# Pools that stay open across the stages of a two-block kernel, and table work on VectorE alone

## The chip, the cores and the metric

The kernel runs on one core of a Trainium2 chip. The metric is the device time of one execution in microseconds, as the median of several runs. Beside it one execution was recorded by the hardware profiler; all rows below are from that one.

The engines are TensorE (PE; its weight loads, PEld, run beside the matmuls), VectorE (DVE), ScalarE (ACT), GpSimd (POOL), and the DMA engines, which here are fed from the queue of SyncE (SP), in order.

## The reference

One sequence of 512 tokens of width 1024, in float32, goes through two blocks one after the other. What matters here:

```python
# first block
sh1, sc1, gt1, sh2, sc2, gt2 = split(silu(c) @ w_ada + b_ada, 6)     # modulation, w_ada is 1024 x 6144
h = rmsnorm(x, norm1_g) * (1 + sc1) + sh1
z = h @ w_in                                                         # q, k, v of three branches, gates, zs
mix = concat(rmsnorm(nsa_attention(...)), rmsnorm(s5_mixer(zs)))     # attention and a state space mixer
x = x + gt1 * (mix @ w_o)
h = rmsnorm(x, norm2_g) * (1 + sc2) + sh2
a, v = split(causal_dwconv(h @ w_up))                                # 2 x 2816 channels
x = rmsnorm(x + gt2 * ((silu(a) * v) @ w_down), normf_g)
# second block
x = x + short_conv_mixer(rms_norm(x))                                # 1024 -> 4 x 2048 -> 1024
x = x + dilated_attention_mixer(rms_norm(x))                         # 3 groups of 16 heads, gate, output
```

The state space mixer needs tables: powers of a complex number per state (`a_re`, `a_im`), products of these with `b` and with `c`.

## The kernel before, in words

**Matrix products.** Every large product is done in three passes on float32r halves: a value is split into a high part (`xh`, `whi`, a copy that rounds, on ScalarE at line 59) and the rest (`xl`, `wlo`, a subtraction on VectorE, line 95 or 358 or 364), and hi x hi, hi x lo, lo x hi are summed in PSUM. `gemm_b` (matmuls at line 128) puts out channels on partitions, `gemm_a` (line 141) tokens. Weights come in pieces of 512 KB through `wload`: `raw` by DMA (line 109), then `whi` and `wlo`, from a pool `wp` with three buffers of each.

**Stages.** First the modulation columns needed for the first norm, the norm, and a projection to the mixer's input (`tables` and `ada_steps`, with eleven buffers of their own); then the mixer's tables and cores, mixed with the projections to q, k and v in the order that the letters in `ORDER` give; then attention over four query tiles (`attend`, "0" to "3"), the gate of the mixer (G), the output projections (`out_s` is w, `out_a` is x) and more halves of the modulation (j n m e h f i) in the order of `ORDER2`. Then the feed-forward part, the short convolution, and the second attention, each in a pool of its own that holds its normed input `xh`, `xl`, its hidden values `hh`, `hl` and the rest, opened where the one before has been closed.

**Who orders what.** A scheduler orders each engine's instructions at build time, by when they would be ready and by priority: as the program is written, unless a `high_priority` block puts them ahead of all others. Only TensorE's order is the program's in two parts (`manual_schedule`). A tile in a pool waits for the last users of the tiles that were there before it.

**The norm between stages.** `residual` adds a finished bank to `x` and, in the last output projection of a stage, sums the squares. `scaled(g)` turns the sums of half g of the tokens into a factor by some ten small VectorE operations (lines 165 to 175 or 313 to 317) and multiplies (line 323) into two tiles of name `adaw`. `norm_t` transposes these on TensorE (line 350) and writes `xh` and `xl`; the first half ahead, the second inside the next stage's first product (`second`). So a stage starts with its first token half while the other is being made. With `first=True` the same is done for the first norm, in eight turns (four pairs of columns, two token halves), each with two writes of `xl`.

**Modulation.** `ada(which)` takes half of a modulation's columns: four pieces of `w_ada` of 512 KB (line 221) through two buffers of name `adaw`, eight matmuls for each (line 223). The same two buffers serve `w_c1` in `hidden` (line 978) and `scaled`.

**Tables.** `cmul` (lines 706 to 721) is a complex product in six operations. From a width of 8 on the imaginary part's three are on GpSimd. Four groups `h` then build `ti` (lines 777 to 788) and `w1` and `w2` (lines 797 to 804), one of the two factors on GpSimd.

Of the kernel before, what the change touches and what calls it, by code (L numbers as in the profile page):

```python
# [26 lines left out]


ORDER = "kvDBCAKc1lbVda0g"
ORDER2 = "032jGn1mehfwxi"  # L30
TC = dict(schedule_with_timeline_sim=True)


# [10 lines left out]
def f(ap):  # L44
    return ap.bitcast(F32)
# [6 lines left out]
def build(tc, A, out, dump=None, stop=None):  # L52
# [15 lines left out]
    with ExitStack() as top:  # L68
# [142 lines left out]
        xss = cst.tile([128, 2, 4, 4], F32, name="xss")  # L211


        def ada_rows(n0, n1, i0, pool, bufs, at):


            pb = bank(at)
            for i, n in ((i0, n0), (i0 + 1, n1)):
                for r in range(2):
                    raw = pool.tile([128, 1024], F32, name="adaw", bufs=bufs)  # L220
                    dma(raw, A["w_ada"][n][:, r * 1024:(r + 1) * 1024])
                    for q in range(4):
                        mm(pb[32 * q:32 * q + 32, :256], csil[:, r * 4 + q, 3 - i:35 - i], raw[:, q * 256:(q + 1) * 256],  # L223
                           start=i == i0 and r == 0, stop=i > i0 and r == 1)
                    yield pb
# [22 lines left out]
        def ada(which):  # L248

            half = which in asum  # L250
            for pb in ada_rows(which * 4 + 2 * half, which * 4 + 2 * half + 1, 2 * half, b1p, 2, acc):
                pass
            if not half:
                asum[which] = sml.tile([128, 256], F32, name="asum", bufs=3)
                V.tensor_copy(asum[which], pb[:, :256])
            else:
                s = asum[which]
                V.tensor_tensor(s, s, pb[:, :256], op=OP.add)
                if which not in (2, 5):
                    ada_cols(s, range(which * 4, which * 4 + 4), pb[:, 256:])  # L260
# [80 lines left out]
        def norm_t(xh, xl, scale, bias, pool, first=False):  # L341

            def turned(g, kp, xn):
                pt = bank(pst)
                for a in range(2):
                    for q in range(2):
                        k = 2 * kp + a
                        nc.tensor.transpose(pt[:, (2 * a + q) * 128:(2 * a + q + 1) * 128],  # L350
                                            xn[q][:, k * 128:(k + 1) * 128], ident)
                for a in range(2):
                    k = 2 * kp + a
                    src = pt[:, a * 256:(a + 1) * 256]
                    tok = slice(g * 256, (g + 1) * 256)
                    if bias is None:
                        act(xh[:, k, tok], src, AF.Copy, scale=scale[:, k:k + 1])
                        V.scalar_tensor_tensor(xl[:, k, tok], src, scale[:, k:k + 1],
                                               f(xh[:, k, tok]), op0=OP.mult, op1=OP.subtract)
                    else:  # L360
                        t = pool.tile([128, 256], F32, name="ntmp", bufs=4)
                        act(t, src, AF.Identity, scale=scale[:, k:k + 1], bias=bias[:, k:k + 1])
                        act(xh[:, k, tok], t)
                        (P if a and first else V).tensor_tensor(xl[:, k, tok], t, f(xh[:, k, tok]), op=OP.subtract)  # L364

            if first:
                xs = x_normed(pool)
                return lambda kp: [turned(g, kp, xs[g]) for g in range(2)]
            half, twice = ahead.pop()

            with tc.high_priority():
                for kp in range(4):
                    turned(0, kp, half[0])

            def second():

                with tc.high_priority():
                    xn, rf = scaled(1, twice)
                for kp in range(4):
                    turned(1, kp, xn)  # L380
                return half[1], rf
            return second
# [67 lines left out]
        divide(8, "acc", "acc", "acc")  # L450


        with ExitStack() as ph:
            ffp = ph.enter_context(tc.tile_pool(name="ffp", bufs=1, reuse_waits="tile"))
            tmp = ph.enter_context(tc.tile_pool(name="fft", bufs=2, reuse_waits="tile"))
            xh = ffp.tile([128, 8, S], F32R, name="xh")
            xl = ffp.tile([128, 8, S], F32R, name="xl")
            hh = ffp.tile([128, 11, S], F32R, name="hh")
            hl = ffp.tile([128, 11, S], F32R, name="hl")
            taps = ffp.tile([128, 44, 4], F32, name="taps")  # L460
            dma(taps, A["conv_taps"].rearrange("p (a b) -> p a b", a=44))
            gf = ffp.tile([128, D], F32, name="gf")
# [34 lines left out]
        with ExitStack() as ph:  # L497
            cvp = ph.enter_context(tc.tile_pool(name="cvp", bufs=1, reuse_waits="tile"))
            tmp = ph.enter_context(tc.tile_pool(name="cvt", bufs=2, reuse_waits="tile"))
            xh = cvp.tile([128, 8, S], F32R, name="xh")  # L500
            xl = cvp.tile([128, 8, S], F32R, name="xl")
            hh = cvp.tile([128, 8, S], F32R, name="hh")
            hl = cvp.tile([128, 8, S], F32R, name="hl")
            taps = cvp.tile([128, 16, 3], F32, name="taps2")
            dma(taps, A["conv_taps_2"].rearrange("p (a b) -> p a b", a=16))

# [40 lines left out]
def block1_mix(tc, nc, E):  # L547
# [158 lines left out]
    def cmul(orr, oi, ar, ai, br, bi, shape):  # L706
# [8 lines left out]
        TT(orr, a1, a2, op=OP.subtract)  # L715
        a1 = tis[0][:, :16 * w].rearrange("p (g w) -> p g w", g=16)
        a2 = tis[1][:, :16 * w].rearrange("p (g w) -> p g w", g=16)
        e = P if w >= 8 else V
        e.tensor_tensor(a1, ar, bib, op=OP.mult)
        e.tensor_tensor(a2, ai, brb, op=OP.mult)  # L720
        e.tensor_tensor(oi, a1, a2, op=OP.add)

    for m in (1, 2, 4):
        cmul(pr[:, :, m + 1:2 * m + 1], pi[:, :, m + 1:2 * m + 1], pr[:, :, 1:m + 1], pi[:, :, 1:m + 1],
# [49 lines left out]
    for h in range(4):  # L774
        g = slice(h * 4, h * 4 + 4)
        for im in range(2):
# [1 line left out]
            w1 = tb.tile([128, 16, 36], F32, name="w1").rearrange("p a b -> p (a b)")[:, :512].rearrange("p (g n c) -> p g n c", g=4, n=8)  # L778
            w2 = tb.tile([128, 16, 36], F32, name="w2").rearrange("p a b -> p (a b)")[:, :512].rearrange("p (g n c) -> p g n c", g=4, n=8)
            a_ = (pi, pr) if im else (pr, pi)  # L780
            for w, b_, p_, e_ in ((w1, bbr, a_[0], V), (w2, bbi, a_[1], P)):
                e_.tensor_tensor(w, b_[:, g, None, :].to_broadcast([128, 4, 8, 16]),
                                 p_[:, g, 0:8, None].to_broadcast([128, 4, 8, 16]), op=OP.mult)
            (P if im else V).tensor_tensor(ti, w1, w2, op=OP.add if im else OP.subtract)
            pt = bank(pss)
            for q in range(4):
                transpose(pt[:, q * 128:(q + 1) * 128], ti[:, q].rearrange("p n c -> p (n c)"), ident)
# [2 lines left out]
    for h in range(4):  # L790
# [5 lines left out]
        for im in range(2):  # L796
            w1 = tb.tile([128, 16, 36], F32, name="w1").rearrange("p a (b c) -> p (a b c)", b=4).rearrange("p (g n c) -> p g n c", g=4, n=9)
            w2 = tb.tile([128, 16, 36], F32, name="w2").rearrange("p a (b c) -> p (a b c)", b=4).rearrange("p (g n c) -> p g n c", g=4, n=9)
            TT(w1, cr_, pi_ if im else pr_, op=OP.mult)
            P.tensor_tensor(w2, ci_, pr_ if im else pi_, op=OP.mult)  # L800
            TT(w1, w1, w2, op=OP.add if im else OP.subtract)
            for par in range(2):
                s = slice(par * 64, par * 64 + 64)
# [433 lines left out]
    dmp("mixl", f(xl))  # L1237
    if stop != "mix":

        E["ahead"].append((E["scaled"](0), False))  # L1240
        out_a(1)
    ctx.close()

# [12 lines left out]
def block2_attn(tc, nc, E):  # L1256
# [15 lines left out]

    with ExitStack() as ph:
        pp = ph.enter_context(tc.tile_pool(name="a2", bufs=1, reuse_waits="tile"))
        yh = pp.tile([128, 8, S], F32R, name="yh")
        yl = Planes([None] * 8)
        xh = pp.tile([128, 8, S], F32R, name="xh")
        xl = pp.tile([128, 8, S], F32R, name="xl")
        second = norm_t(xh, xl, cols[:, 24:32], None, None)

        wz = wload(A["w_z"][0], 8, 256)
# [11 lines left out]
        dma(gains, A["qk_gain"])  # L1293
        TS(gains[:, 0:3], gains[:, 0:3], -0.125, None, op0=OP.mult)

        kbh = [pp.tile([128, 4, 2, 128], F32R, name=f"kbh{i}") for i in range(2)]
        kbl = [pp.tile([128, 4, 2, 128], F32R, name=f"kbl{i}") for i in range(2)]
        for t in kbh + kbl:
            P.memset(f(t), 0.0)
        md = dr.tile([512, 4], F32, name="md")  # L1300
        wd = dr.tile([512, 2], F32, name="wd")

# [460 lines left out]
```

## Time and profile before

| | us |
|---|---|
| median of 3 runs | 1817.91 (1816.0 to 1825.29) |
| the profiled execution | 1823.86 |
| its span, first to last instruction | 1822.1 |
| TensorE busy in the span | 1751.0 |
| VectorE busy | 1095.5 |
| ScalarE busy | 845.7 |
| GpSimd busy | 184.3 |

A "busy" TensorE has an instruction in it; its granted clock is listed beside it, 1.00 being the full 2.4 GHz. The profiler's span starts at 0; all times in the rows are from there. Idle time is named by what ended it: "[3.80 <-DVE adaw L323]" says that the engine stood 3.80 us until VectorE's instruction of line 323 had written `adaw`.

### The profile page before, as it was taken

What the parts mean: (1) busy time and instruction counts of PE and PEld (TensorE: products, weight loads), DVE (VectorE), ACT (ScalarE), POOL (GpSimd) and SP (SyncE); (2) the same over time, 40 slices, a digit from 0 to 9 for tenths busy, and PEclk for the clock granted to TensorE, in tenths of its full rate; (3) what the DMA queues carried; (4) which work ended last, traced back from release to release, by engine and by line L of the source; (5) the groups of instructions that cost most, each with busy time, mean ns of one, the idle gap of its engine ahead of it and who ended that gap; (6) DMA issues with size and microseconds to landing.
All of it is one profiled execution on the core that took longest, in us unless ns stands there. A gap on an engine that the chain in (4) does not pass through costs nothing.

```text
span 1822.1 us, 25899 instructions
## 1 busy us (share of the span) xinstructions
PE 1751.0 (96%) x9588; PEld 1441.2 (79%) x9588; DVE 1095.5 (60%) x2720; ACT 845.7 (46%) x1679; POOL 184.3 (10%) x179
## 2 busy tenths in 40 slices
PE   5899989999999999899999999999999999999999
PEld 3787746888888888788888888878888888888877
DVE  8895766865545557643333333644766766666676
ACT  3532656564423445532322323445655655656653
POOL 3764202001100110000000000000000000000000
PEclk9998999999999999999999999999999999999999
DMA  8357750332333335333333323533222322322221
GB/s 341 95 152 199 230 176 12 102 122 92 94 92 104 95 102 173 106 104 95 102 93 99 98 93 104 152 107 102 85 78 82 94 73 80 91 74 91 82 65 64
DMA packets 86782, 200.21 MB, mean 110 GB/s; under 512 B 32000, under 2 KB 36864, under 8 KB 86656
## 3 DMA queue, kind: packets, MB, share of 16 engines
q1 hardware_dynamic: 86656, 198.57, 35.3%
q8 instruction: 75, 1.23, 0.3%
q14 instruction: 51, 0.42, 0.1%
HBM read 193.75 MB, written 4.78 MB: 109 GB/s over the span
## 4 chain that ended last, share of the span: by engine, by line
PE 85%; DVE 7%; DMA 4%; ACT 2%; issue 1%; POOL 1%; SPq 0%; DVEq 0%; ACTq 0%; POOLq 0%
PE bank L128 38%; PE bank L141 35%; DMA adaw<-in_w_ada_dram 2%; DVE wlo L95 1%; PE bank L1163 1%; PE bank L1500 1%; PE bank L1470 1%; PE bank L1580 1%; PE bank L223 1%; PE bank L1159 1%; PE bank L1558 1%; PE bank L1140 1%; PE bank L1569 1%; PE bank L1587 1%; ACT whi L59 1%
## 5 line engine op out<-in xcount | busy, mean ns | idle before, releaser
L95 DVE TENSOR_TENSOR wlo<-raw,whi 128x1024 fp32r<-128x1024 f32 (+1 forms) x287 | 350.1, 1220 | 302.5 <-ACT whi L59 288.5
L59 ACT ACTIVATE whi<-raw 128x1024 fp32r<-128x1024 f32 (+1 forms) x287 | 299.4, 1043 | 473.7 <-PE bank L128 265.2
L128 PE MATMUL bank<-xh,whi 128*128 128x512 f32 (+1 forms) x1120 | 291.2, 379 | 10.7 <-ACT xh L59 10.6
L128 PE MATMUL bank<-xl,whi 128*128 128x512 f32 (+1 forms) x1120 | 288.3, 375 | 7.0 <-DVE xl L364 6.8
L128 PE MATMUL bank<-xh,wlo 128*128 128x512 f32 (+1 forms) x1120 | 283.6, 374 | 0.0
L128 PEld LDWEIGHTS bank<-xh,whi 128*128 128x128 f32 x1120 | 204.3, 191 | 52.8 <-ACT xh L59 13.8
L128 PEld LDWEIGHTS bank<-xl,whi 128*128 128x128 f32 x1120 | 203.9, 189 | 47.1 <-DVE xl L364 8.8
L128 PEld LDWEIGHTS bank<-xh,wlo 128*128 128x128 f32 x1120 | 202.4, 189 | 37.7
L141 PE MATMUL bank<-whi,xh 128*128 128x512 f32 (+2 forms) x800 | 209.2, 361 | 2.5 <-ACT v L59 1.2
L141 PE MATMUL bank<-wlo,xh 128*128 128x512 f32 (+2 forms) x800 | 205.1, 356 | 0.0
L141 PE MATMUL bank<-whi,xl 128*128 128x512 f32 (+2 forms) x800 | 204.9, 355 | 0.0
L141 PEld LDWEIGHTS bank<-wlo,xh 128*128 128x128 f32 x800 | 135.5, 190 | 22.5 <-issue 1.6
L141 PEld LDWEIGHTS bank<-whi,xl 128*128 128x128 f32 x800 | 135.2, 190 | 22.5 <-issue 1.6
L141 PEld LDWEIGHTS bank<-whi,xh 128*128 128x128 f32 x800 | 128.8, 189 | 21.2 <-issue 3.9
L141 PE MATMUL bank<-wlo,hh 128*128 128x512 f32 x304 | 95.0, 389 | 0.0
L141 PE MATMUL bank<-whi,hl 128*128 128x512 f32 x304 | 94.9, 389 | 0.0
L198 DVE SCALAR_TENSOR_TENSOR cy<-bank,taps,cy 128x384 f32<-128x384 f32 (+3 forms) x176 | 72.9, 477 | 32.5 <-ACT cy L59 32.5
L59 ACT ACTIVATE P<-P,stat 128x128 f32<-128x128 f32 (+1 forms) x192 | 79.8, 419 | 21.9 <-DVE stat L1478 15.7
L141 PE MATMUL bank<-whi,hh 128*128 128x512 f32 x304 | 89.8, 389 | 0.0
L534 POOL TENSOR_TENSOR cy<-cy,sz 128x512 f32<-128x512 f32 x16 | 28.8, 1801 | 436.5 <-ACT sz L59 436.5
L141 PEld LDWEIGHTS bank<-whi,hl 128*128 128x128 f32 x304 | 57.1, 188 | 11.9
L141 PEld LDWEIGHTS bank<-wlo,hh 128*128 128x128 f32 x304 | 57.0, 188 | 11.8
(384 smaller groups left out, 2322.3 us busy)
## 6 DMA issues: line engine op xcount, KB each, us to landing
raw<-in_conv_w_in_dram SPq DMA_DIRECT2D x64, 512.0 KB, 3.7
raw<-in_w_pair_dram SPq DMA_DIRECT2D x64, 512.0 KB, 3.8
adaw<-in_w_ada_dram SPq DMA_DIRECT2D x48, 512.0 KB, 5.1
raw<-in_w_up_dram SPq DMA_DIRECT2D x44, 512.0 KB, 3.7
raw<-in_w_down_dram SPq DMA_DIRECT2D x30, 512.0 KB, 3.5
raw<-in_conv_w_out_dram SPq DMA_DIRECT2D x24, 512.0 KB, 3.7
raw<-in_w_o_dram SPq DMA_DIRECT2D x12, 512.0 KB, 4.2
x<-in_x_dram SPq DMA_DIRECT2D x8, 512.0 KB, 5.2
```

Of the source, the lines that this page charges most:

```text
L59: return nc.scalar.activation(o, i, fn, **kw)
L95: (eng or V).tensor_tensor(lo, src, f(hi), op=OP.subtract)
L128: mm(ps[:, tok], a[:, q, j * 128:(j + 1) * 128], b[:, k0 + q, tok], start=n == 0 and i == 0 and h != 1, stop=n == len(w) - 1 and i == 3 * ...
L141: mm(ps, a[:, base + k0 + q, tok], b[:, q, :], start=first and n == 0 and i == 0 and o == 0, stop=last and n == len(w) - 1 and i == 3 * kn ...
L198: V.scalar_tensor_tensor(o, i, t, o, op0=OP.mult, op1=OP.add)
L223: mm(pb[32 * q:32 * q + 32, :256], csil[:, r * 4 + q, 3 - i:35 - i], raw[:, q * 256:(q + 1) * 256], start=i == i0 and r == 0, stop=i > i0 ...
L534: P.tensor_tensor(y, y, sz, op=OP.mult)
L1140: mm(ps[:, :n], qs[:, h, qt], kk[:, br, kvh, 0:n], start=kk is ksh, stop=kk is ksl)
L1159: transpose(pt[:, s * 128:(s + 1) * 128], prs[hl][:, j * 128:(j + 1) * 128], ident)
L1163: mm(po[par * 64:par * 64 + 64, kvh * 256:(kvh + 1) * 256], vsw[:, j, br, kvh * 64:kvh * 64 + 64], ptt[:, par, :], start=False, stop=br == ...
L1470: mm(ps[:, :nk * 256], a[:, natural(i)], b[:, j0:i + 1].rearrange("p j h k -> p (j h k)"), start=n == 0, stop=n == 2)
L1500: mm(ps[:, r * 256:(r + 1) * 256], a[:, natural(2 * rr + r)], b[:, 2 * rr + r].rearrange("p h k -> p (h k)"), start=n == 0, stop=n == 2)
```

## The change

Six things are done:

- `xh`, `xl` of the three later stages come from one pool `nx` and `hh`, `hl` (eight planes each) from one pool `hp`, both open from the end of the first block's mixer to the end. The feed-forward part's last three planes are tiles of its own. The second attention uses `hh`'s tile for `yh` and `hl`'s for its four block matrices, zeroed by one instruction.
- The second of each pair of `w_ada` pieces in `ada` goes through `wp`'s `raw` buffers.
- In `ORDER2` the half i stands in front of w and x.
- `scaled(0)` in front of `out_a(1)` has high priority.
- All `xl` of the first norm are made by VectorE, with high priority.
- `cmul` and the tables run on VectorE alone.

```diff
-ORDER2 = "032jGn1mehfwxi"
+ORDER2 = "032jGn1mehfiwx"
...
-        def ada_rows(n0, n1, i0, pool, bufs, at):
+        def ada_rows(n0, n1, i0, pool, bufs, at, more=None):
...
-                    raw = pool.tile([128, 1024], F32, name="adaw", bufs=bufs)
+                    raw = more.tile([128, 1024], F32, name="raw") if more and r else \
+                        pool.tile([128, 1024], F32, name="adaw", bufs=bufs)
...
-            for pb in ada_rows(which * 4 + 2 * half, which * 4 + 2 * half + 1, 2 * half, b1p, 2, acc):
+            for pb in ada_rows(which * 4 + 2 * half, which * 4 + 2 * half + 1, 2 * half, b1p, 2, acc, W["p"]):
...
-                        (P if a and first else V).tensor_tensor(xl[:, k, tok], t, f(xh[:, k, tok]), op=OP.subtract)
+                        with tc.high_priority() if first else nullcontext():
+                            V.tensor_tensor(xl[:, k, tok], t, f(xh[:, k, tok]), op=OP.subtract)
...
+        hp = top.enter_context(tc.tile_pool(name="hp", bufs=1, reuse_waits="tile"))
+        nx = top.enter_context(tc.tile_pool(name="nx", bufs=1, reuse_waits="tile"))
+
+        def hidden():
+            return [hp.tile([128, 8, S], F32R, name=n) for n in ("h0", "h1")]
+
+        def normed():
+            return [nx.tile([128, 8, S], F32R, name=n) for n in ("nxh", "nxl")]
...
-            xh = ffp.tile([128, 8, S], F32R, name="xh")
-            xl = ffp.tile([128, 8, S], F32R, name="xl")
-            hh = ffp.tile([128, 11, S], F32R, name="hh")
-            hl = ffp.tile([128, 11, S], F32R, name="hl")
+            xh, xl = normed()
+            hh, hl = (Planes([h[:, k] for k in range(8)] + [ffp.tile([128, S], F32R, name=f"{n}{k}") for k in range(3)])
+                      for n, h in zip(("hh", "hl"), hidden()))
...
-            xh = cvp.tile([128, 8, S], F32R, name="xh")
-            xl = cvp.tile([128, 8, S], F32R, name="xl")
-            hh = cvp.tile([128, 8, S], F32R, name="hh")
-            hl = cvp.tile([128, 8, S], F32R, name="hl")
+            xh, xl = normed()
+            hh, hl = hidden()
...
-        e = P if w >= 8 else V
-        e.tensor_tensor(a1, ar, bib, op=OP.mult)
-        e.tensor_tensor(a2, ai, brb, op=OP.mult)
-        e.tensor_tensor(oi, a1, a2, op=OP.add)
+        TT(a1, ar, bib, op=OP.mult)
+        TT(a2, ai, brb, op=OP.mult)
+        TT(oi, a1, a2, op=OP.add)
...
-            for w, b_, p_, e_ in ((w1, bbr, a_[0], V), (w2, bbi, a_[1], P)):
-                e_.tensor_tensor(w, b_[:, g, None, :].to_broadcast([128, 4, 8, 16]),
+            for w, b_, p_ in ((w1, bbr, a_[0]), (w2, bbi, a_[1])):
+                TT(w, b_[:, g, None, :].to_broadcast([128, 4, 8, 16]),
...
-            (P if im else V).tensor_tensor(ti, w1, w2, op=OP.add if im else OP.subtract)
+            TT(ti, w1, w2, op=OP.add if im else OP.subtract)
...
-            P.tensor_tensor(w2, ci_, pr_ if im else pi_, op=OP.mult)
+            TT(w2, ci_, pr_ if im else pi_, op=OP.mult)
...
-        E["ahead"].append((E["scaled"](0), False))
+        with tc.high_priority():
+            E["ahead"].append((E["scaled"](0), False))
...
-        yh = pp.tile([128, 8, S], F32R, name="yh")
+        yh, kb = E["hidden"]()
...
-        xh = pp.tile([128, 8, S], F32R, name="xh")
-        xl = pp.tile([128, 8, S], F32R, name="xl")
+        xh, xl = E["normed"]()
...
-        kbh = [pp.tile([128, 4, 2, 128], F32R, name=f"kbh{i}") for i in range(2)]
-        kbl = [pp.tile([128, 4, 2, 128], F32R, name=f"kbl{i}") for i in range(2)]
-        for t in kbh + kbl:
-            P.memset(f(t), 0.0)
+        P.memset(f(kb), 0.0)
+        kbs = [kb[:, 2 * i:2 * i + 2].rearrange("p a (b h k) -> p (a b) h k", b=2, h=2) for i in range(4)]
+        kbh, kbl = kbs[0:2], kbs[2:4]
```

## Rows read from the trace of the kernel before

**Rows 1.** The page: busy time of the engines, and the chain that ended last.
```profile
PE 1751.0 (96%) x9588; PEld 1441.2 (79%) x9588; DVE 1095.5 (60%) x2720; ACT 845.7 (46%) x1679; POOL 184.3 (10%) x179
...
PE 85%; DVE 7%; DMA 4%; ACT 2%; issue 1%; POOL 1%; SPq 0%; DVEq 0%; ACTq 0%; POOLq 0%
```

**Rows 2.** Stretches: length, busy by engine, granted clock, DMA share, GB/s.
```profile
20.00:105.00 85.00, 72.90 (x525) 55.94 (x526) 75.23 (x144) 40.88 (x77) 55.24 (x48) 1.00 0.50 169
105.00:200.00 95.00, 87.67 (x756) 76.58 (x757) 67.84 (x123) 29.86 (x69) 45.73 (x51) 0.91 0.72 199
200.00:262.00 62.00, 54.85 (x396) 32.69 (x394) 45.77 (x174) 36.42 (x96) 5.92 (x8) 1.00 0.61 205
...
340.00:384.00 44.00, 39.22 (x325) 36.86 (x325) 38.22 (x104) 24.29 (x60) 0.00 (x0) 0.96 0.53 170
...
745.00:770.00 25.00, 17.00 (x121) 16.10 (x121) 15.58 (x42) 13.29 (x28) 0.00 (x0) 0.86 0.20 62
...
1194.00:1216.00 22.00, 18.50 (x124) 16.49 (x123) 11.72 (x33) 9.32 (x21) 3.64 (x4) 0.92 0.24 79
```

**Rows 3.** Timeline of VectorE at 23 to 46: start, length, line, operation.
```profile
23.60 0.43 DVE L364 TENSOR_TENSOR xl<-ntmp,xh 128x256 fp32r<-128x256 f32 x1
...
28.20 1.22 DVE L95 TENSOR_TENSOR wlo<-raw,whi 128x1024 fp32r<-128x1024 f32 x1
...
45.84 0.68 DVE L782 TENSOR_TENSOR w<-bbr,pi 128x512 f32<-128x512 f32 x1
```

**Rows 4.** VectorE's groups by form, 20 to 105: busy, mean ns, idle before.
```profile
L95 DVE TENSOR_TENSOR wlo<-raw,whi 128x1024 fp32r<-128x1024 f32 x9 | 14.0, 1553 | 0.2 <-ACT whi L59 0.2
...
L364 DVE TENSOR_TENSOR xl<-ntmp,xh 128x256 fp32r<-128x256 f32 x8 | 7.2, 907 | 0.3 <-ACT xh L59 0.3
L782 DVE TENSOR_TENSOR w<-bbr,pr 128x512 f32<-128x512 f32 x4 | 4.5, 1114 | 2.5 <-POOL ti L784 2.5
```

**Rows 5.** TensorE's waits, whole span: us in total, times, longest.
```profile
PE bank L128 <- DVE xl L364: 6.8, 4, 2.5
...
PE bank L981 <- DMA adaw<-in_w_c_dram: 3.0, 1, 3.0
```

**Rows 6.** TensorE's waits in the stretch 200 to 262.
```profile
PE bank L223 <- DMA adaw<-in_w_ada_dram: 6.8, 8, 1.5
```

**Rows 7.** The load queue (SP), 205 to 262.
```profile
218.97 41.18 SPq L221 DMA_DIRECT2D adaw<-in_w_ada_dram  x15
```

**Rows 8.** Timeline into the feed-forward part, 360 to 380.
```profile
363.20 0.15 DVE L307 TENSOR_REDUCE nss<-xss 128x2 f32<-128x8 f32 x1
...
371.72 0.88 DVE L406 SCALAR_TENSOR_TENSOR rtmp<-bank,rs_yo,gt 128x256 f32<-128x256 f32 x2
...
374.58 1.42 DVE L323 TENSOR_SCALAR adaw<-x,rs_yn 128x1024 f32<-128x1024 f32 x2
...
375.48 3.28 PE L350 MATMUL bank<-ident,adaw 128*128 128x128 f32 x16 [3.80 <-DVE adaw L323]
```

**Rows 9.** Timeline into the convolution, 730 to 768.
```profile
732.36 1.47 PE L350 MATMUL bank<-ident,adaw 128*128 128x128 f32 x12
...
750.96 0.46 ACT L59 ACTIVATE xh<-bank,cols 128x256 fp32r<-128x256 f32 x1
...
751.47 1.22 PE L128 MATMUL bank<-xh,whi 128*128 128x256 f32 x4 [6.27 <-ACT xh L59]
...
751.83 0.48 DVE L358 SCALAR_TENSOR_TENSOR xl<-bank,cols,xh 128x256 fp32r<-128x256 f32 x1
...
757.37 1.42 DVE L323 TENSOR_SCALAR adaw<-x,rs_ym 128x1024 f32<-128x1024 f32 x2
...
763.72 1.91 PE L350 MATMUL bank<-ident,adaw 128*128 128x128 f32 x16
```

**Rows 10.** Timeline into the second attention, 1196 to 1204.
```profile
1198.86 0.17 DVE L1294 TENSOR_SCALAR qkg<-qkg 128x3 f32<-128x3 f32 x1 [1.96 <-DMA qkg<-in_qk_gain_dram]
...
1200.26 0.75 PE L128 MATMUL bank<-xh,whi 128*128 128x256 f32 x4 [2.15 <-ACT xh L59]
```

## The prediction

> **What bounds the kernel now.** I read the page first, then stretches, then waits, then the stages where they collect. TensorE is busy 1751.0 of 1822.1 us and 85% of the chain that ended last is its matmuls [rows 1]: most of the span is matrix work that this change doesn't touch. What it can move is the 71.1 us in which TensorE is idle, and the time at the lower clock. The table of stretches [rows 2] says where they lie: 12.1 us idle in 20 to 105 (tables, first norm, first projection), 7.3 in 105 to 200 with a granted clock of 0.91, 7.2 in 200 to 262 (attention with the modulation weights), 4.8 in 340 to 384 (into the feed-forward part), 8.0 in 745 to 770 (into the convolution), 3.5 in 1194 to 1216 (into the second attention). The first 20 us are the first load and stay. The rows also show VectorE at 75.23 of 85 us in the first stretch with GpSimd at 55.24 beside it, so moving GpSimd's work there isn't free by itself.
>
> **Tables and first norm on VectorE.** By the code 40 GpSimd operations move: each of the norm's eight turns gives one of its two `xl` to GpSimd (a=1), 8 in all; 8 of `w2` and 4 of `ti` with 512 columns; 8 of `w2` with 576; and 12 of `cmul` (three each at 128, 256 and 512 columns, three at 256 for `bbi`). On a free VectorE 256 columns take 0.43 us and 512 take 0.68 [rows 3]; from these I estimate 0.3 for 128 and 0.77 for 576. Sum: 8 x 0.43 + 12 x 0.68 + 8 x 0.77 + 3 x (0.3 + 0.43 + 0.68 + 0.43) = 23.3 us more for VectorE.
> Against it stands a refund. The same forms run longer while GpSimd runs: the `xl` take 0.907 on average where 0.43 was possible, the weight splits 1.553 for 1.22, the first `w1` 1.114 for 0.68 [rows 3, 4]. That is 8 x 0.48 + 9 x 0.33 + 4 x 0.43 = 8.5 us from three groups alone; the other groups are not all shown, so 8.5 is the least and 23.3 (each moved operation already costs VectorE its length today) the most. VectorE also stops waiting for GpSimd (2.5 us before the `w1` group [rows 4]) and has 85 - 75.23 = 9.8 us idle.
> A rule of the Trainium skill bears on it (SBUF — State Buffer, Who interferes with whom): a VectorE instruction with two SBUF inputs and a GpSimd instruction that reads SBUF use one shared read interface, and the later one blocks for the whole length of the other. By that rule the refund is near its upper end and the price near nothing; the rows above would then give a gain of the 6.8 us named next.
> What it does to TensorE: four waits for `xl` cost 6.8 us [rows 5]. The half of `xl` on VectorE stands behind table work there, and the other half behind GpSimd's slower copy of it. With all on VectorE in front of the tables these go. Bounds: -6.8 if the tables end no later; at the other end 23.3 - 8.5 - 9.8 = +5.0, if the least refund is all there is and the tables' consumers wait for it. I take -3, nearer to the gain, since three groups of many already refund a third.
>
> **More load buffers.** `ada` loads four 512 KB pieces a half through two buffers; now every second piece takes one of the three `raw` buffers of the weight loads. In 200 to 262 TensorE waits 6.8 us in eight places for these pieces [rows 6], and the load queue issues 15 of them over 41.18 us [rows 7], one each time a buffer is given back, while the DMA engines are 61% busy [rows 2]. With four or five in flight most waits should go. Bounds: -6.8, and 0 if the softmax between them only moves up to be the next wait. I take -5. Work stays the same; only issue times move. The queue is SP's, in order: a piece that waits for a `raw` buffer holds the weight loads behind it. In 200 to 262 only `w_o` pieces, needed later, are behind; in 105 to 200 (half l) the loads of `w_in_g`, `w_glu` and `w_c` are. There the wait of 3.0 us for `w_c`, which shares the two buffers with l's four pieces [rows 5], should go as l needs two of them. Bounds: -6 (the wait and as much again of the work done at the lower clock in that stretch [rows 2]) and +3 (the same wait, moved to a weight load). I take -2.
> The half i moved ahead of `out_s` and `out_a` costs the same matmuls and loads; it is covered by the same attention work and frees the two buffers that `scaled` needs.
>
> **Into the feed-forward part.** The scale chain starts at 363.20 and its last operation at 374.58: 11.4 us for some ten operations of 0.2 us, because residuals and splits lie between. TensorE's transposes wait 3.80 us for it [rows 8]. At high priority it is done before 370. Next late is the last read of the old PSUM banks, 371.72 + 0.88 = 372.6, which the newly divided PSUM must wait for and this change leaves. So 375.48 moves to 372.6: -2.9, I take -3. Bounds: 0 (a third wait) and -5 (if the 3.28 us for 16 transposes, done in 1.91 elsewhere [rows 8, 9], also falls).
>
> **Into the convolution.** The first token half is transposed by 733.8, but ScalarE writes `xh` only at 750.96, past the last matmul of the down projection, and TensorE stands 6.27 us [rows 9]. `xh` comes from a pool opened where the feed-forward pool is closed; with `nx` kept, only the up projection's matmuls read those bytes before, and by the code they are done before the second down projection starts. Then the first half's matmuls run right behind, and the end is set by the second half: its scaling ends at 757.37 + 1.42, with eight `xl` of 0.48 us, which now are done earlier, in front [rows 9]. 758.8 - 3.8 = 755.0, and 763.72 moves there: -8.7. The least is -3 (half of the 6.27, if the chain of residuals moves no earlier). I take -7, since another 1 to 2 us may stay in the queue order.
>
> **Into the second attention.** TensorE's wait of 2.15 us follows VectorE's 1.96 us for the load of `qkg` [rows 10], a tile in a pool that now begins elsewhere, on bytes free long before. PSUM is divided again here as before, so the transposes still start after the last residual. I take -2, bounds 0 and -4. The one zeroing of `kb` is off the path: its first reader comes some 20 us later.
>
> **The sum.** -3 - 5 - 2 - 3 - 7 - 2 = -22. The profiled execution took 1823.86 us, 1822.1 of it span; 1801.9 is expected of it. The median shown is 1817.91, 5.95 below this execution, so 1817.91 - 22 = 1795.9: I say 1796. All bounds at their best give -6.8 - 6.8 - 6 - 5 - 8.7 - 4 = -37 (1781), all at their worst +5 + 0 + 3 + 0 - 3 + 0 = +5 (1823).
>
> **Rivals.**
> A. As summed, 0.62: 1796, own range 1786 to 1806.
> B. All waits go and the clock stays up, 0.12: 1781. For it speaks the refund and that TensorE is full outside these stretches; against it that each wait has a next one.
> C. The boundaries alone bring something, 0.15: tables and loads hand their gain to VectorE's softmax (45.77 of 62 us busy in 200 to 262 [rows 2]). -3 - 7 - 2 = -12: 1806.
> D. The kept pools do nothing, 0.07: `xh` is late since ScalarE's queue has the squares and splits in front of it, not for its memory. Then 7 and 2 are missing: -13, 1805. Against it: ScalarE writes `xh` directly behind work that waits for the last matmul, 17 us after the transposes.
> E. Slower, 0.04: VectorE saturates. No refund and no usable idle time: the tables end 23.3 us later, TensorE stands behind them at `kq` and the block matrices, and does as much work after it at the lower clock, at which 16 transposes took 3.28 us for 1.91 [rows 8, 9]: 23.3 x (1 - 1.91 / 3.28) = 9.7 us lost. 23.3 + 9.7 - 12 - 5 = +16: 1834. It decides from the point where the tables are over 17 us late, the 12 and 5 of the other gains; with the least refund and the idle time they are 5.0 late. The Trainium skill has a rule that would favour it (Perfetto Trace Analysis, Optimizing Scalar/DVE Operations): where VectorE is saturated, giving work to GpSimd may pay. It adds itself that the two share a read port, so that it might not; the rows on the refund agree with that.
>
> **Chances.** 0.5% (9.1 us, 1808.8) is about what a measurement of this kernel can tell from no change. A, B and most of C and D lie below it: faster 0.85, same 0.11, slower 0.04. The range leaves out part of B below and part of C, D and E above: 1782 to 1809.
>
> **What would show it.** Right: the waits for `xl` and for the modulation pieces gone from the waits of TensorE; `xh` of the convolution written directly behind its transposes, some 10 us ahead of the down projection's last matmul rather than 6 behind it; TensorE's idle time near 745 down to 1 to 3 us; forms on VectorE at 0.43, 0.68 and 1.22 us up to where rope's GpSimd work begins. Wrong: VectorE over 80 of 85 us in the first stretch with a new wait of TensorE for `kq` or `ti`, SP's queue standing on a `raw` buffer in 105 to 200, or `xh` still behind the last matmul.

## The result and the profile after

The changed kernel takes 1795.38 us, median of four runs (1790.6 to 1801.5), against 1821.6 for the kernel before beside it (four runs, 1816.0 to 1826.2): a ratio of 0.9852, 95% interval 0.9828 to 0.9875, or 26.2 us less. The profiled execution of after is the slowest of its four (1801.5 us, span 1799.7); against the profiled one of before (span 1822.1) it is 22.4 us shorter. Executions of one kernel differ by some 10 us: of after's four the fastest had a granted clock of 0.995 over its span and the slowest, the profiled one, 0.988 (before's profiled one 0.991).

The page of after, busy time of the engines and the chain that ended last; they answer to [rows 1]:
```profile
PE 1742.1 (97%) x9588; PEld 1440.5 (80%) x9588; DVE 1095.9 (61%) x2760; ACT 843.4 (47%) x1679; POOL 134.7 (7%) x136
...
PE 86%; DVE 8%; ACT 2%; DMA 2%; issue 1%; SPq 0%; POOL 0%; DVEq 0%; ACTq 0%
```
VectorE executes 40 instructions more than before and is busy 0.4 us more: all the work moved to it is paid back.

The stretches of after, columns as in [rows 2]; the last three are the same boundaries, 13, 19 and 22 us earlier than in before:
```profile
20.00:105.00 85.00, 78.30 (x617) 61.21 (x618) 81.98 (x198) 44.48 (x86) 8.04 (x8) 0.90 0.54 185
105.00:200.00 95.00, 87.56 (x711) 76.50 (x703) 65.75 (x132) 28.45 (x66) 44.52 (x52) 0.91 0.70 207
200.00:262.00 62.00, 59.51 (x464) 37.43 (x463) 45.80 (x171) 37.52 (x99) 5.83 (x8) 0.97 0.64 216
327.00:371.00 44.00, 37.92 (x299) 37.68 (x298) 39.18 (x106) 24.81 (x61) 0.00 (x0) 0.92 0.42 126
726.00:751.00 25.00, 21.33 (x150) 19.44 (x149) 15.84 (x39) 12.76 (x24) 0.00 (x0) 1.00 0.37 107
1172.00:1194.00 22.00, 19.75 (x136) 17.55 (x135) 13.78 (x34) 10.33 (x22) 3.52 (x1) 1.00 0.33 106
```
TensorE gains in all stretches but two. From 105 to 200 it idles as long as before. Into the feed-forward part (327 to 371) it idles 6.1 us where it idled 4.8. The granted clock from 20 to 105 was 0.90 here and 1.00 in before, so that some of the busy time in that stretch is slower matmuls; their number still rose from 525 to 617.

VectorE's groups by form in 20 to 105 of after, against [rows 4]:
```profile
L95 DVE TENSOR_TENSOR wlo<-raw,whi 128x1024 fp32r<-128x1024 f32 x11 | 14.5, 1317 | 0.3 <-ACT whi L59 0.3
...
L366 DVE TENSOR_TENSOR xl<-ntmp,xh 128x256 fp32r<-128x256 f32 x16 | 6.0, 418 | 0.0
...
L790 DVE TENSOR_TENSOR w<-bbr,pr 128x512 f32<-128x512 f32 x4 | 2.8, 692 | 0.1
```
Sixteen `xl` now cost VectorE 6.0 us, where eight cost 7.2 before.

TensorE's waits over the whole span of after, and in a second view those from 200 to 262, against [rows 5, 6]:
```profile
PE bank L224 <- DMA adaw<-in_w_ada_dram: 14.9, 5, 12.2
PE bank L351 <- DVE adaw L324: 8.4, 2, 6.1
PE bank L989 <- DMA adaw<-in_w_c_dram: 2.8, 1, 2.8
PE bank L128 <- ACT nxh L59: 2.7, 4, 1.0
```
```profile
PE bank L224 <- DMA adaw<-in_w_ada_dram: 2.3, 2, 1.3
```
The waits for `xl` are gone (0.2 us left of 6.8), and those for modulation pieces in attention fell from 6.8 to 2.3. The wait for `w_c` is as long as before (2.8, before 3.0), but not the same one (below), and the one for `adaw` into the feed-forward part grew.

The timeline into the feed-forward part of after, against [rows 8]:
```profile
350.57 0.15 DVE L308 TENSOR_REDUCE nss<-xss 128x2 f32<-128x8 f32 x1
...
357.46 1.23 DVE L95 TENSOR_TENSOR wlo<-raw,whi 128x1024 fp32r<-128x1024 f32 x1 [0.97 <-ACT whi L59]
...
358.60 0.48 DVE L408 SCALAR_TENSOR_TENSOR rtmp<-bank,rs_yo,gt 128x256 f32<-128x256 f32 x1
...
361.52 1.41 DVE L324 TENSOR_SCALAR adaw<-x,rs_yn 128x1024 f32<-128x1024 f32 x2
...
362.41 3.64 PE L351 MATMUL bank<-ident,adaw 128*128 128x128 f32 x16 [6.08 <-DVE adaw L324]
```
The scale chain still takes 11 us from its first operation (350.57) to its last (361.52). TensorE's last matmul ended at 356.3, and the reading of its bank stands behind a weight split that itself waits for ScalarE.

The timelines into the convolution (first three) and into the second attention (last), against [rows 9, 10]:
```profile
719.53 1.47 PE L351 MATMUL bank<-ident,adaw 128*128 128x128 f32 x12
...
720.06 1.57 ACT L59 ACTIVATE nxh<-bank,cols 128x256 fp32r<-128x256 f32 x4
...
743.33 2.10 PE L351 MATMUL bank<-ident,adaw 128*128 128x128 f32 x16 [2.33 <-DVE adaw L324]
```
```profile
1178.02 0.50 PE L128 MATMUL bank<-nxh,whi 128*128 128x256 f32 x2 [0.46 <-ACT nxh L59]
```
`nxh` is written right behind its transposes, not 17 us later. Four marks divide the gain of the two profiled executions: the transposes into the feed-forward part are 13.1 us earlier (375.48 to 362.41), the first ones into the convolution 12.8 (732.36 to 719.53), the second ones 20.4 (763.72 to 743.33), and the second attention's first matmul 22.2 (1200.26 to 1178.02). By the prediction's terms these are 13, 13, 20 and 22.

### The profile page after: what moved, and what is told of

Same layout as the page of the kernel before. It is cut to its first block, busy times and chain, and to the rows that moved or that the text cites. A ratio compares the mean times of both kernels' runs of the same rounds, so it can differ in the third digit from the quotient of the medians.

```text
span 1799.7 us, 25866 instructions
## 1 busy us (share of the span) xinstructions
PE 1742.1 (97%) x9588; PEld 1440.5 (80%) x9588; DVE 1095.9 (61%) x2760; ACT 843.4 (47%) x1679; POOL 134.7 (7%) x136
## 4 chain that ended last, share of the span: by engine, by line
PE 86%; DVE 8%; ACT 2%; DMA 2%; issue 1%; SPq 0%; POOL 0%; DVEq 0%; ACTq 0%
PE bank L128 38%; PE bank L141 36%; DVE wlo L95 1%; PE bank L1477 1%; PE bank L1171 1%; PE bank L1507 1%; PE bank L1148 1%; PE bank L1587 1%; PE bank L1167 1%; PE bank L1565 1%; ACT whi L59 1%; DVE h L1462 1%; PE bank L1576 1%; PE bank L1594 1%; DMA adaw<-in_w_ada_dram 1%
## 5 line engine op out<-in xcount | busy, mean ns | idle before, releaser
L128 PE MATMUL bank<-nxh,whi 128*128 128x512 f32 (+1 forms) x1072 | 273.2, 375 | 2.7 <-ACT nxh L59 2.7
L128 PE MATMUL bank<-nxl,whi 128*128 128x512 f32 (+1 forms) x1072 | 271.8, 373 | 0.0
L128 PE MATMUL bank<-nxh,wlo 128*128 128x512 f32 (+1 forms) x1072 | 269.3, 373 | 0.0
L128 PEld LDWEIGHTS bank<-nxh,whi 128*128 128x128 f32 x1072 | 194.8, 189 | 39.4 <-ACT nxh L59 3.8
L128 PEld LDWEIGHTS bank<-nxl,whi 128*128 128x128 f32 x1072 | 194.4, 188 | 35.8
L128 PEld LDWEIGHTS bank<-nxh,wlo 128*128 128x128 f32 x1072 | 193.4, 188 | 35.5
L141 PE MATMUL bank<-whi,nxh 128*128 128x512 f32 x512 | 164.3, 401 | 1.2 <-ACT v L59 1.1
L141 PE MATMUL bank<-whi,h 128*128 128x512 f32 x576 | 160.4, 391 | 0.0
L141 PE MATMUL bank<-whi,nxl 128*128 128x512 f32 x512 | 158.7, 391 | 0.0
L141 PE MATMUL bank<-wlo,nxh 128*128 128x512 f32 x512 | 158.3, 390 | 0.0
L141 PEld LDWEIGHTS bank<-whi,h 128*128 128x128 f32 x576 | 107.5, 188 | 22.2 <-issue 0.2
```

The lines of the kernel that those rows point to most:

```text
L128: mm(ps[:, tok], a[:, q, j * 128:(j + 1) * 128], b[:, k0 + q, tok], start=n == 0 and i == 0 and h != 1, stop=n == len(w) - 1 and i == 3 * ...
L141: mm(ps, a[:, base + k0 + q, tok], b[:, q, :], start=first and n == 0 and i == 0 and o == 0, stop=last and n == len(w) - 1 and i == 3 * kn ...
```

## The experiments

Times are medians, ratios are to the kernel before measured beside each kernel, and a difference to after is taken to its 1795.38. The kernel before itself came out between 1820.42 and 1823.53 in the rounds of the experiments, so that a difference to after of under 3 us says nothing.

**One part alone.** Three kernels carry one part of the change each.

e1, only the work moved to VectorE:
```
-                        (P if a and first else V).tensor_tensor(xl[:, k, tok], t, ...)
+                        with tc.high_priority() if first else nullcontext():
+                            V.tensor_tensor(xl[:, k, tok], t, ...)
-        e = P if w >= 8 else V
-        e.tensor_tensor(a1, ar, bib, op=OP.mult)
+        TT(a1, ar, bib, op=OP.mult)
...
```


> The kernel before with only the table and first-norm operations moved from GpSimd to VectorE (and the first norm's xl ahead in the order). Full refund (the two engines only took each other's time): VectorE's forms at 0.42, 0.68 and 1.22 us, TensorE's projection begins 8 us earlier (before 74.20, after 65.75) and the whole is 5 to 8 us faster. Part refund, as the prediction summed: 3 us faster. Given back: the projection begins earlier, but the wait for w_c and the work at the lower clock behind it take it back by 195 us, and the whole is within 2 us of before.

1818.18 us against 1823.53, ratio 0.9969 (0.9956 to 0.9983). The projection begins at 64.33, 9.9 us earlier than in before, but the transposes into the feed-forward part only 5.3 earlier (370.15): half is given back on the way, and from 200 to 262 TensorE still waits 6.1 us for modulation pieces, at a granted clock of 0.86. The full refund holds: 40 instructions more on VectorE cost it 1.2 us (1095.5 before, 1096.7 here).

e2, only the kept pools:
```
-            xh = ffp.tile([128, 8, S], F32R, name="xh")
-            xl = ffp.tile([128, 8, S], F32R, name="xl")
+            xh, xl = normed()
...
```


> The kernel before with only the kept pools (normed and hidden tiles, one zeroing of kb). Boundaries set by the opening of a pool: xh of the convolution is written right behind its transposes, the wait of 6.27 us goes, TensorE's wait for qkg of 2.15 us goes, and the whole is 7 to 10 us faster. Rival, ScalarE's own order holds xh back: the 6.27 us stay and the whole is within 2 us of before.

1813.07 us, ratio 0.9946 (0.9928 to 0.9965). The timeline of this kernel into the convolution:
```profile
729.02 1.57 ACT L59 ACTIVATE nxh<-bank,cols 128x256 fp32r<-128x256 f32 x4
...
752.29 2.10 PE L350 MATMUL bank<-ident,adaw 128*128 128x128 f32 x16 [2.33 <-DVE adaw L323]
```
With nothing else changed `nxh` is written from 729.02 on, 12 us ahead of the end of the down projection (741.2), and the 6.27 us are gone. What is left, 2.33, is the second half's scale chain. Rival D (ScalarE's order) falls.

e3, only the load buffers, half i's place and the priority:
```
-ORDER2 = "032jGn1mehfwxi"
+ORDER2 = "032jGn1mehfiwx"
-                    raw = pool.tile([128, 1024], F32, name="adaw", bufs=bufs)
+                    raw = more.tile([128, 1024], F32, name="raw") if more and r else \
+                        pool.tile([128, 1024], F32, name="adaw", bufs=bufs)
...
```


> The kernel before with only the raw buffers for the modulation weights, half i ahead of out_s and out_a, and scaled(0) at high priority. By the prediction's terms: 10 us faster (5 in attention, 2 for w_c, 3 into the feed-forward part). By the marks of the two profiles: 9 us gained by the end of attention, 2 to 3 lost again into the feed-forward part, where TensorE's wait for adaw grows from 3.8 to about 6; the whole 5 to 7 us faster. Rival, the softmax takes the place of the loads: 0 to 3 us faster.

1813.45 us, ratio 0.9942 (0.9921 to 0.9964): 10.1 us, the prediction's sum for this part, though not by its terms. TensorE's waits over the whole span in this kernel:
```profile
PE bank L351 <- DVE adaw L324: 6.1, 1, 6.1
...
PE bank L982 <- DMA adaw<-in_w_c_dram: 2.5, 1, 2.5
```
The waits for modulation pieces from 200 to 262 fall by 5.0 to 1.8, a wait for `w_c` is there as in after, and the one into the feed-forward part grows by 2.3 with this part alone. These waits make up less than half of the 10.1; where the rest lies isn't settled. The three parts give 5.4, 10.5 and 10.1, together 25.9; the whole change gave 26.2. They add up.

**What the tables' gain is made of.** e5 moves only the first norm's `xl` (first lines of e1's diff), e6 only the table work (the rest). The high priority around `xl` doesn't put them in front, here or in e1 or after: the kernel compiled without it is the same, instruction for instruction. So e5 tests the engine of half of the `xl`, and no run tests their place in the order.

> The kernel before with only the first norm's xl all on VectorE and ahead in the order; the table work stays on GpSimd. If the gain of the tables part comes from the two engines no longer lengthening each other: VectorE's xl stay near 0.9 us (0.907 before), its weight splits near 1.5, only part of TensorE's 6.8 us of waits for xl goes, and the whole is 1 to 3 us faster. Rival, the place of xl in the order does it: the 6.8 us go and the whole is 5 to 6 us faster, as with the tables moved too.

1824.82 us against 1821.73, ratio 1.0028 (1.0010 to 1.0045): slower. VectorE's `xl` in 20 to 105, TensorE's waits there, and from the timelines of before and of e5 the last `xl`, which in both stand right behind the table product `w<-bbr,pi`:
```profile
L365 DVE TENSOR_TENSOR xl<-ntmp,xh 128x256 fp32r<-128x256 f32 x16 | 12.7, 818 | 0.0
```
```profile
PE bank L128 <- DVE xl L365: 7.7, 5, 2.9
```
```profile
66.18 2.15 DVE L364 TENSOR_TENSOR xl<-ntmp,xh 128x256 fp32r<-128x256 f32 x2
```
```profile
66.61 4.33 DVE L365 TENSOR_TENSOR xl<-ntmp,xh 128x256 fp32r<-128x256 f32 x4
```
All on VectorE, each still takes 0.818 while GpSimd does table work, and TensorE waits 7.7 us for them, not less than the 6.8 of before.

> The kernel before with only the table work moved to VectorE; the first norm keeps every second xl on GpSimd. If the engines lengthen each other: VectorE's forms fall to 0.43 to 0.5 for xl, 1.25 for the weight splits and 0.68 for 512 columns, VectorE's busy time in the first 105 us does not rise by more than 4 us, and the whole is 3 to 5 us faster. Rival, the place of xl: TensorE's waits for xl stay at 5 to 7 us and the whole is within 1 us of before.

1814.52 us, ratio 0.9967 (0.9952 to 0.9982): all of e1's gain. TensorE's waits for `xl` from 20 to 105 in this kernel:
```profile
PE bank L128 <- DVE xl L364: 3.1, 3, 1.8
PE bank L128 <- POOL xl L364: 2.4, 1, 2.4
```
`xl` on VectorE falls only to 0.687, not to the expected 0.43 to 0.5, with the other half still on GpSimd, and 5.5 us of waits are left. So the gain is in the table work's engine; but it is there although most of the waits for `xl` stay, and these go only with both moved (e1, after). How the gain reaches TensorE in e6 isn't settled.

**The load buffers.** e9 is after with `more` left out of the call of `ada_rows`.
```
-            for pb in ada_rows(..., b1p, 2, acc, W["p"]):
+            for pb in ada_rows(..., b1p, 2, acc):
```


> The kernel after without the raw buffers for the modulation weights (two buffers again, half i still moved ahead). If the buffers bring the gain of the loads part (10.1 us alone): TensorE's waits for modulation pieces are back at 18 to 20 us with the start, and the whole is 8 to 11 us slower than after, about 1805. Rival, the moved half i brings it: the whole within 2 us of after.

1810.23 us, 14.9 more than after. TensorE's waits for modulation pieces are 18.6 with the start, 5.9 of them from 200 to 262 (after: 2.3), and the wait into the feed-forward part is 6.81. The buffers carry the gain of their part, though the waits for pieces explain only 3.6 of it. 14.9 is more than the 10.1 of the part alone; whether half i's new place costs the difference when it has two buffers, no run separates.

**Into the feed-forward part.** e4 is after with half i back in its old place.
```
-ORDER2 = "032jGn1mehfiwx"
+ORDER2 = "032jGn1mehfwxi"
```


> The kernel after with half i put back behind out_s and out_a(0). If i's matmuls and its place covered the scale chain: TensorE's wait for adaw into the feed-forward part falls from 6.08 to 4 us or less, and the whole is 2 to 3 us faster than after. Rival, VectorE's order makes the wait (a weight split that waits for ScalarE stands in front of the last reading of PSUM, 2.2 us): the wait stays at 5 to 6 us and the whole is within 1 us of after, or 2 us slower if i's last load then comes late.

1795.61 us, as after. The timeline of this kernel:
```profile
352.52 0.87 DVE L408 SCALAR_TENSOR_TENSOR rtmp<-bank,rs_yo,gt 128x256 f32<-128x256 f32 x2
...
353.53 3.43 PE L351 MATMUL bank<-ident,adaw 128*128 128x128 f32 x16 [4.73 <-DVE rtmp L408]
```
Here the first half's scaling is done at 351.2, and the transposes wait for the last reading of PSUM instead, as the prediction had it; but that reading stands 3.7 us behind the last matmul (348.8), in VectorE's queue. The wait is 1.4 us shorter than in after and the whole no faster.

e7 puts the split of the first up-projection weight on GpSimd; e8 does so with half i in its old place.
```
-            wa, wb = wload(w0, 8, 256), wload(w1, 8, 256)
+            wa, wb = wload(w0, 8, 256, eng=eng), wload(w1, 8, 256)
...
-                        both = gemm_two(xh, xl, A["w_up"][0], A["w_up"][1], second)
+                        both = gemm_two(xh, xl, A["w_up"][0], A["w_up"][1], second, P)
```


> The kernel after with the split of the first up-projection weight (two pieces) on GpSimd, so that VectorE reads the last banks of the out-projection without a weight split in front. If VectorE's queue makes the wait into the feed-forward part: TensorE's wait for adaw falls from 6.08 to 3 to 4 us, and the whole is 2 to 3 us faster than after (1793 where after has 1795). Rival, the scale chain's own length makes it: the wait stays above 5 us. A third way: GpSimd's splits are late and TensorE waits for wlo instead, the whole 2 us slower.

1795.13 us, as after, with the wait at 6.58. The timeline of this kernel says why:
```profile
342.83 5.26 POOL L95 TENSOR_TENSOR wlo<-raw,whi 128x1024 fp32r<-128x1024 f32 x2 [27.96 <-DVE rs_mn L175]
...
343.36 2.38 DVE L165 TENSOR_SCALAR rs_yn<-rs_mn 128x2 int32<-128x2 int32 x1
...
345.77 2.34 DVE L168 TENSOR_TENSOR rs_un<-rs_yn 128x2 f32<-128x2 f32 x1
```
Two operations of the scale chain on two columns, 0.16 and 0.15 us in after, take 2.38 and 2.34 beside GpSimd's two splits (5.26 together). The queue got shorter by two splits and the chain longer by more; the experiment doesn't separate its theories.

> The same with half i put back behind out_s and out_a(0). There the scale chain is done early and TensorE waits for the last reading of PSUM (4.73 us for rtmp). If VectorE's queue makes that: the wait falls to 1 to 2 us, and the whole is 3 us faster than after. Rival: one split still stands ahead of the last reading and the wait stays at 4 us, the whole as after.

1800.52 us, 5 more than after, the wait 7.27: two operations of the chain took 2.37 and 2.27 in the same way.

e12 takes four splits, those of the first two up-projection weights, off VectorE without GpSimd. It leaves the low parts out: copies of the weights stand in their place.
```
-                (eng or V).tensor_tensor(lo, src, f(hi), op=OP.subtract)
+                if eng is nc.scalar:
+                    act(lo, src)
+                else:
+                    (eng or V).tensor_tensor(lo, src, f(hi), op=OP.subtract)
...
+            wa, wb = wload(w0, 8, 256, eng=eng), wload(w1, 8, 256, eng=eng)
...
+                        both = gemm_two(xh, xl, A["w_up"][0], A["w_up"][1], second, nc.scalar)
```


> The kernel after, with the low parts of the first two up-projection weights (four pieces) not subtracted on VectorE but written by ScalarE as copies of the weight, so that part of the feed-forward result isn't the reference's. It takes four splits of 1.22 us off VectorE around the end of the out-projection, with nothing on GpSimd. If VectorE, busy 11.18 of the last 11.6 us of the out-projection, makes TensorE's wait into the feed-forward part: the wait falls from 6.08 to 3 to 4 us and the whole is 2 to 3 us faster than after. Rival, the length of the scale chain and of the residual makes it: the wait stays within 1 us of 6. The other side: ScalarE's four copies of 1.06 us hold back the squares, and the wait grows.

1789.66 us, ratio to before 0.9819 (0.9802 to 0.9836), 5.7 less than after, whose interval (0.9828 to 0.9875) it just overlaps. The timeline of this kernel:
```profile
346.92 1.42 DVE L327 TENSOR_SCALAR adaw<-x,rs_yn 128x1024 f32<-128x1024 f32 x2
...
347.82 3.38 PE L354 MATMUL bank<-ident,adaw 128*128 128x128 f32 x16 [2.65 <-DVE adaw L327]
```
The wait is 2.65, and VectorE is busy 9.87 of the last 11.7 us of the out-projection. The weight splits in VectorE's queue made more than half of the wait: without four of them the chain, a dozen operations, takes 7.5 us (339.41 to 346.92) and not 11. Whether the splits hold it back by their length or by standing in front, where one also waits 0.97 for ScalarE, e12 doesn't separate. The 3.4 us of the wait are more than half of the 5.7; where the rest lies isn't settled.

**Further along the same road.** e10 takes rope's 16 additions off GpSimd too, e11 also 24 operations of the state-space core (its expectation counted 20) and 6 of gelu.
```
-            P.tensor_tensor(ot, ta[:, t, :, None, :].to_broadcast(sh_), ...)
+            V.tensor_tensor(ot, ta[:, t, :, None, :].to_broadcast(sh_), ...)
...
-        P.tensor_tensor(s2, zi, ei, op=OP.mult)
+        V.tensor_tensor(s2, zi, ei, op=OP.mult)
...
```


> The kernel after with the 16 additions of rope (19.3 + 3.2 us on GpSimd) on VectorE too. If GpSimd's two-operand work costs VectorE its own length wherever it runs: VectorE's busy time in the mix stage rises by less than the 10 us that the 16 additions take on it (12 of 0.68 and 4 of 0.42), and the whole is 2 to 4 us faster than after (1791 to 1793). Rival, what is refunded there isn't on the path, since VectorE waits for ScalarE in that stretch: within 1.5 us of after. The other side: VectorE's queue gets longer in front of the keys and the whole is 3 us slower.

1790.62 us, ratio 0.9837 (0.9817 to 0.9856), 4.8 less than after. Its interval overlaps after's too.

> The same with the state-space core's 20 additions and products (some 17 us on GpSimd) and the 6 products of gelu on VectorE as well. Refund theory: 3 to 8 us faster than after (1787 to 1792), the scan on VectorE (0.945 mean) and the xs (0.606) shorter. Rival, off the path: within 2 us of after. The other side: VectorE saturates between 105 and 160 us and the whole is 3 to 6 us slower.

1789.30 us, ratio 0.9825 (0.9806 to 0.9844), 6.1 less than after. The page of this kernel, and from another view its stretch from 105 to 200:
```profile
PE 1734.7 (97%) x9588; PEld 1436.8 (80%) x9588; DVE 1098.5 (61%) x2806; ACT 846.0 (47%) x1679; POOL 87.6 (5%) x90
```
```profile
105.00:200.00 95.00, 90.68 (x733) 79.74 (x730) 75.03 (x198) 35.23 (x82) 6.23 (x11) 0.93 0.68 201
```
46 instructions more than after cost VectorE 2.6 us, and TensorE is busy 3.1 us more of this stretch, in the one profiled execution of each. Its scan falls from 0.945 to 0.674 and `xs` from 0.606 to 0.420. All four runs (1788.42 to 1789.72) lie below all four of after, but the intervals of the two ratios overlap, so that the size of the further gain isn't settled.

## Why the prediction was right, and where it wasn't

It said 1796 and 1795.38 was measured. The sum of -22 is that of the two profiled executions (-22.4); the medians give -26.2. That the median came out within 1 us is luck: the kernel before, 1817.91 in the prediction, measured 1821.6 with one execution more, and 3.7 us more at the start met 4.2 us more of gain.

- **Tables and first norm, -3.** Right in sign, mis-sized: -5.4 alone, inside the bounds. The refund isn't the 8.5 of three groups but nearly all of the moved work: 40 instructions cost VectorE 1.2 us in e1 and 0.4 in after, where 23.3 was the price summed. The way it was to come was wrong: "With all on VectorE in front of the tables these go". They don't stand in front, since the high priority changes no order, and on VectorE alone they are slower than before (e5). The waits go only when GpSimd's tables and its `xl` are both moved, and most of them can stay without the gain being less (e6).
- **Load buffers in attention, -5.** Right for the waits, which fell by 4.5. The buffers are worth more than their waits (e9: 14.9), by a way that isn't settled.
- **`w_c` in 105 to 200, -2.** "The wait of 3.0 us for `w_c` ... should go": that one did, but nothing was won. TensorE's products with `w_c` in before (first line) and in after:
```profile
152.94 1.97 PE L981 MATMUL bank<-adaw,wk 128*64 128x256 f32 x8 [2.99 <-DMA adaw<-in_w_c_dram]
```
```profile
112.15 1.98 PE L989 MATMUL bank<-adaw,wk 128*64 128x256 f32 x8 [2.81 <-DMA adaw<-in_w_c_dram]
...
146.24 1.95 PE L989 MATMUL bank<-adaw,wk 128*64 128x256 f32 x16 [0.76 <-issue]
```
The second call of `hidden`, behind half l, begins at 152.94 in before and waits for its load; in after it begins at 146.24 with its first two pieces there. In its place a wait of 2.81 stands in the first call, ahead of l, where before had none; e1 has one of 3.0 there and e3 one of 2.5, so that either part alone brings it. The step that failed is that no other wait would follow: the stretch idles 7.4 us, before 7.3, at the same granted clock of 0.91. What the prediction named as a sign of being wrong was there: between 85 and 160 us the load queue stands 8.6 us on `raw` buffers that a weight split must give back, before it can issue modulation pieces. No wait of TensorE for such a piece came of it in that stretch.
- **Into the feed-forward part, -3.** The step that failed most: "At high priority it is done before 370." Without the high priority the compiled kernel has the same instructions in the same order on every engine, so that this edit does nothing; it was not run. What did act was half i's new place, which the prediction put at no cost: its 32 matmuls no longer stretch the out-projection, VectorE is busy 11.18 of its last 11.6 us (before: 9.62), and the chain spreads over 11 us as before but ends 6 us behind the last matmul, not 4. With i in its old place the wait is 4.73 with the `raw` buffers (e4) and 3.80 and 3.83 without them (e1, e2), in its new place 6.08 and 6.81 (after, e9). e12 shows that the splits in VectorE's queue make more than half of it.
- **Into the convolution, -7, and the second attention, -2.** Right: 7.6 and 1.9 between the marks, and 10.5 for the pools alone. The granted clock of the stretch into the convolution is 1.00, before 0.86, and part of the gain may be that. The bound of -8.7 wasn't reached: TensorE still waits 2.33 us for the second half's scaling, whose chain follows the last residual.
- **The rivals.** C falls with e1 and e3, D with e2, E with the page: VectorE was over the 80 us named as a sign of saturation (81.98 of 85), yet no wait of TensorE for `kq` came with it and none over 0.4 us at `ti`'s transposes, since more of the work now lies in that stretch. B falls with the waits that are left and with the clock, 0.90 and 0.91 in the two stretches up to 200.

The sum held because terms that were too small stood against two that failed: by the end of the out-projection after is 15.3 us ahead (its last matmul there ends at 356.33, before at 371.68), where the first three terms gave 10, and it then loses 2.3 where 3 were to be won.

## What to carry to other kernels

Elementwise work with two operands on GpSimd beside a busy VectorE isn't free: here 40 instructions that kept GpSimd busy for 48 us cost VectorE 1.2 us in all when they moved to it (e1), so try all of it on VectorE. A tile of a pool that was opened with its stage was written 17 us late here, and the same tile of a kept pool at once, so keep buffers of one shape across stages. Before work is moved away from a boundary, see whether it was the slack in which another engine finished. See whether an edit of priority changes the order at all: neither of the two here did. And when a wait is named by its engine and line, look where it stands: here the sum stayed while one wait went and another came.

## What the runs showed of the hardware

The size of the interference was not expected. An operation on 128x2 elements took 0.16 us in after and 2.38 in e7, as long as what was left of GpSimd's running subtraction (5.26 for two). In all four places, two in e7 and two in e8, VectorE stood until GpSimd's instruction ended, however short its own was. This agrees with the Trainium skill (SBUF — State Buffer, Who interferes with whom), by which whichever of the two engines takes their shared pair of ports first has it for the whole instruction, and the other fully blocks. The prediction gave that rule's result as a gain of 6.8 us and took 3; e1 measured 5.4.
